# Neighbourhood attention in a two-layer diffusion backbone: value products of two blocks side by side, TensorE in the order of the code, projections spread over the blocks

## The chip, the core and the metric

The kernel runs on one core of one Trainium2 chip. The core has engines that run beside each other, each with its own queue of instructions, kept in step by semaphores: TensorE (PE; its weight loads stand in the profile as PEld), VectorE (DVE), ScalarE (ACT), GpSimd (POOL) and SyncE (SP), which here only issues DMAs. The metric is the device time of one execution in microseconds (us), lower is better. Three runs of the kernel before gave 2879.36, 2881.08 and 2881.36 us, median 2881.08 us.

## What is computed

The reference is a backbone of two layers over 1024 latent tokens (a grid of 16 rows and 64 columns) and 256 context tokens, width 1024. Each layer mixes tokens in two groups of eight heads, an mLSTM and a neighbourhood attention, and then has an MLP. The change touches the neighbourhood attention alone:

```python
def row_block(r):
    rs = jnp.clip(r - kr_n // 2, 0, rows - kr_n)          # 8 rows of keys
    q_r = lax.dynamic_index_in_dim(qg, r, axis=2, keepdims=False)
    k_r = lax.dynamic_slice_in_dim(kg, rs, kr_n, axis=2)
    v_r = lax.dynamic_slice_in_dim(vg, rs, kr_n, axis=2)
    s_loc = einsum(q_r, k_r) + bias                        # 16 columns of keys each
    s_ctx = einsum(q_r, kch)                               # and all 256 context tokens
    p = softmax(concatenate([s_loc, s_ctx], -1))
    return einsum(p_loc, v_r) + einsum(p_ctx, vch)
```

In the first layer the 256 context tokens also attend among themselves (`need_ctx`); in the last layer they do not.

## The kernel before

All products are fp32, or fp32 split into a high and a low half, so that a product with a weight matrix is three matmuls (`mm3`, lines 84 to 88: high by high, high by low, low by high). A projection of one group of tokens (`qk_project`, lines 704 to 710) is 8 steps over the width of three matmuls each, so 24 matmuls; the context group has 256 columns, each of the two latent groups 512.

**Blocks.** The attention goes through the heads in four pairs (`pr` 0 to 3). A latent block is 128 queries (8 rows by 16 columns) of both heads of a pair; its keys are the 256 context tokens and a window of 11 or 12 rows by 24 or 32 columns. A pair of heads has 8 latent blocks, and in the first layer 2 context blocks ahead of them: 10 blocks a pair there, 8 in the second layer, 72 in all.

**A block's three steps** (`na_block`, lines 845 to 905, a generator with two `yield`s):

1. Scores. PE: 4 matmuls against the context keys (line 853) and 4 against the window (line 863). DVE takes them out of PSUM with a running minimum of the negated scores (lines 858 and 864; 864 adds the bias that a DMA put into the tile `S`). ACT does the exponential and the row sum (868), DVE the reciprocal (869) and the scaling (870).
2. Transposes. PE turns the probabilities: 4 for the context (878), 4 and 2 for the window (889, 897). ACT copies the first and the last out of PSUM (879, 898), DVE the middle ones (890, tile `pl`).
3. Values. PE: 10 matmuls (904), each with 64 columns of weights, the two heads into the two halves of one PSUM bank. DVE copies the result out (784, or 761 for a context block; tile `nyT`).

**The order of the code.** `na` (lines 816 to 843) keeps two blocks pending. For each new block it asks for the transposes of the older pending one, then for the new block's scores, then for one step of `nxt`, and then for the values of the oldest block. `nxt` is the next pair's `na_qk` (712 to 746): a step of it is one projection of keys or queries of one group, 6 steps in the first layer and 5 in the second, taken one a block until none is left. For the last pair `nxt` is `ahead` (790 to 805): four steps that load and split output weights and load attention results, two that load residuals, and four output tiles of 24 matmuls. PSUM has 8 banks: 2 for projections (`mm`), 6 for all else (`q`), and each block takes 6 of the latter in turn.

**What sets the order on the engines.** The code's order is only what a scheduler starts from: before the program is built it reorders the instructions of every engine by estimated times, so that pieces of a projection may stand between a block's steps. A tile's buffers are handed round; a DMA into `S` (6 buffers, line 772) or into `vt` (the values of a window, line 776) is issued by SP, in SP's own order, when the last reader of that buffer is done.

## Time and profile before

The profiled execution has a span of 2883.5 us on its one core; it is 2.4 us above the median of the three runs without profile.

| engine | busy us | instructions |
|---|---|---|
| PE (matmuls) | 2833.7 | 16644 |
| PEld (weight loads) | 2402.4 | 16644 |
| DVE | 2216.7 | 5097 |
| ACT | 1262.9 | 2426 |
| POOL | 67.3 | 117 |

The attention stage runs from 457 to 688 us in the first layer and from 1963 to 2181 us in the second, 449 us in all. How to read it: an engine's busy time says little here about what sets the end, since PE's matmuls are pipelined and their ends are modelled. The sharper reading is the distance from the start of one matmul to the start of the next in the timeline. A timeline row gives start, time until the last of the merged instructions ended, engine, line, operation, output<-inputs, shape and count; `128*64 128x128` means 64 columns of weights.

### The profile page before, as it was taken

What the parts mean: (1) busy time and instruction counts of PE and PEld (TensorE: products, weight loads), DVE (VectorE), ACT (ScalarE), POOL (GpSimd) and SP (SyncE); (2) the same over time, 40 slices, a digit from 0 to 9 for tenths busy, and PEclk for the clock granted to TensorE, in tenths of its full rate; (3) what the DMA queues carried; (4) which work ended last, traced back from release to release, by engine and by line L of the source; (5) the groups of instructions that cost most, each with busy time, mean ns of one, the idle gap of its engine ahead of it and who ended that gap; (6) DMA issues with size and microseconds to landing.
All of it is one profiled execution on the core that took longest, in us unless ns stands there. A gap on an engine that the chain in (4) does not pass through costs nothing. (4 is left out here: it accounts for less than half of the span.)

```text
span 2883.5 us, 45724 instructions
## 1 busy us (share of the span) xinstructions
PE 2833.7 (98%) x16644; PEld 2402.4 (83%) x16644; DVE 2216.7 (77%) x5097; ACT 1262.9 (44%) x2426; POOL 67.3 (2%) x117
## 2 busy tenths in 40 slices
PE   8999999999999999999999999999999999999998
PEld 5888888888888888888889988888878788888888
DVE  7789987885798777599877778877786887759774
ACT  5333334564553333344544333335565533334453
POOL 0000000001000000000000000000010000000000
PEclk9999999999999999999999999999999999999999
DMA  7433332246447555798977222223256454478673
GB/s 248 164 123 105 113 115 78 91 125 217 150 157 235 188 197 198 273 334 288 313 260 252 67 88 73 74 62 105 88 169 199 132 190 144 154 252 312 212 252 102
DMA packets 278946, 497.42 MB, mean 173 GB/s; under 512 B 23328, under 2 KB 119584, under 8 KB 278720
## 3 DMA queue, kind: packets, MB, share of 16 engines
q1 hardware_dynamic: 278720, 494.49, 51.7%
q8 instruction: 131, 2.15, 0.3%
q14 instruction: 95, 0.78, 0.1%
HBM read 398.82 MB, written 95.59 MB: 171 GB/s over the span
## 5 line engine op out<-in xcount | busy, mean ns | idle before, releaser
L86 PE MATMUL q<-ah,whi 128*128 128x512 f32 (+1 forms) x1480 | 551.8, 373 | 2.6 <-ACT ah L955 1.9
L88 PE MATMUL q<-ah,wlo 128*128 128x512 f32 (+1 forms) x1480 | 550.2, 372 | 1.3 <-DVE wlo L956 1.3
L87 PE MATMUL q<-al,whi 128*128 128x512 f32 (+1 forms) x1480 | 550.7, 372 | 0.0
L86 PE MATMUL mm<-ah,whi 128*128 128x512 f32 (+1 forms) x1112 | 382.8, 344 | 1.5 <-ACT ah L914 1.5
L87 PE MATMUL mm<-al,whi 128*128 128x512 f32 (+1 forms) x1112 | 382.4, 344 | 0.4 <-DVE al L915 0.4
L88 PE MATMUL mm<-ah,wlo 128*128 128x512 f32 (+1 forms) x1112 | 382.1, 344 | 0.5 <-DVE wlo L81 0.5
L86 PEld LDWEIGHTS q<-ah,whi 128*128 128x128 f32 x1480 | 278.8, 188 | 52.3 <-ACT ah L955 2.7
L88 PEld LDWEIGHTS q<-ah,wlo 128*128 128x128 f32 x1480 | 278.8, 188 | 51.3 <-DVE wlo L956 2.1
L87 PEld LDWEIGHTS q<-al,whi 128*128 128x128 f32 x1480 | 278.9, 188 | 48.9 <-issue 1.4
L86 PE MATMUL mm<-whi,ah 128*128 128x512 f32 (+2 forms) x864 | 313.3, 364 | 0.9 <-DVE st L312 0.4
L87 PE MATMUL mm<-wlo,ah 128*128 128x512 f32 (+2 forms) x864 | 309.5, 359 | 0.2 <-DVE wlo L81 0.2
L88 PE MATMUL mm<-whi,al 128*128 128x512 f32 (+2 forms) x864 | 308.2, 357 | 0.0
L86 PEld LDWEIGHTS mm<-ah,whi 128*128 128x128 f32 x1112 | 210.5, 189 | 27.9 <-ACT ah L914 1.9
L88 PEld LDWEIGHTS mm<-ah,wlo 128*128 128x128 f32 x1112 | 210.6, 189 | 25.6 <-DVE wlo L81 1.0
L87 PEld LDWEIGHTS mm<-al,whi 128*128 128x128 f32 x1112 | 210.5, 189 | 25.0 <-DVE al L915 0.5
L955 ACT CAST ah<-raw 128x512 fp32r<-128x512 f32 (+1 forms) x264 | 142.9, 566 | 120.7 <-PE q L88 58.3
L86 PEld LDWEIGHTS mm<-whi,ah 128*128 128x128 f32 x864 | 163.6, 190 | 28.0 <-issue 3.1
L88 PEld LDWEIGHTS mm<-whi,al 128*128 128x128 f32 x864 | 163.8, 190 | 23.0 <-issue 0.7
L87 PEld LDWEIGHTS mm<-wlo,ah 128*128 128x128 f32 x864 | 163.9, 190 | 22.3 <-DVE wlo L81 0.4
L956 DVE TENSOR_TENSOR al<-raw,ah 128x512 fp32r<-128x512 f32 (+1 forms) x264 | 157.6, 621 | 23.5 <-ACT ah L955 23.0
L956 DVE TENSOR_TENSOR wlo<-raw,whi 128x1024 fp32r<-128x1024 f32 x84 | 102.4, 1222 | 74.4 <-ACT whi L955 71.9
L86 PE MATMUL q<-th,whi 128*128 128x512 f32 x384 | 150.5, 392 | 2.2 <-DVE s L1120 2.0
(287 smaller groups left out, 5249.4 us busy)
## 6 DMA issues: line engine op xcount, KB each, us to landing
raw<-w SPq DMA_DIRECT2D x168, 512.0 KB
raw<-hid SPq DMA_DIRECT2D x104, 512.0 KB
wada<-w_adaT SPq DMA_DIRECT2D x96, 512.0 KB
wraw<-w SPq DMA_DIRECT2D x80, 512.0 KB
hid<-hb SPq DMA_DIRECT2D x128, 256.0 KB
hid<-ht SPq DMA_DIRECT2D x96, 256.0 KB
gb<-gscr SPq DMA_DIRECT2D x36, 512.0 KB
wada<-w_ada SPq DMA_DIRECT2D x32, 512.0 KB
```

Source lines behind the costliest of these rows:

```text
L86: mm(out, lh, rh, start=start, stop=False, skip_group_check=True)
L87: mm(out, lh, rl, start=False, stop=False, skip_group_check=True)
L88: mm(out, ll, rh, start=False, stop=stop, skip_group_check=True)
L955: ins = self.nc.scalar.copy(hi, src)
L956: self.nc.vector.tensor_sub(lo, src, fview(hi))
```

## The change

The order of the code in the attention is new, and on PE it is kept as written:

- `na_pairs` goes through the blocks two by two. While the two blocks of a pair are scored, each scoring is preceded by the transposes of one block of the pair behind; when both are scored, the values of both blocks behind are asked for, one after the other (20 matmuls in one run).
- It runs under `manual_schedule` for PE: PE's instructions keep the code's order. DVE, ACT, POOL and SP are still ordered by the scheduler.
- A step of the next pair's projections is taken where `(n + 1) * parts // blocks` grows: in the first layer with the blocks n = 1, 3, 4, 6, 8, 9 (of 0 to 9), in the second with n = 1, 3, 4, 6, 7 (of 0 to 7). Before, these were the first 6 and the first 5 blocks. In the last pair `nxt` is stepped as before: the output tiles come with n = 8 and 9 in the first layer, 6 and 7 in the second, and at the end.
- `vt` has 5 buffers in place of 3.

```diff
-                vt = np_.tile([128, 3, 128], F32, name="vt", bufs=3)
+                vt = np_.tile([128, 3, 128], F32, name="vt", bufs=5)
...
-        pending = []
+        with self.tc.manual_schedule(engines={mybir.EngineType.PE}):
+            self.na_pairs(l, hi, lo, need_ctx, last)
+
+    def na_pairs(self, l, hi, lo, need_ctx, last):
+
+        behind, pair = [], []
+        parts, blocks = (6, 10) if need_ctx else (5, 8)
         for pr in range(4):
             nxt = self.na_qk(l, pr + 1, hi, lo, need_ctx) if pr < 3 else last
             for n, blk in enumerate(self.na_blocks(l, pr, need_ctx)):
-                if len(pending) == 2:
-                    next(pending[0])
+                if behind:
+                    next(behind[n % 2])
                 next(blk)
-                pending.append(blk)
-
-                if pr < 3 or not need_ctx or n > 1:
+                pair.append(blk)
+
+                if (n + 1) * parts // blocks > n * parts // blocks if pr < 3 else not need_ctx or n > 1:
                     next(nxt, None)
-                if len(pending) > 2:
-                    run_all(pending.pop(0))
+                if len(pair) == 2:
+                    for b in behind:
+                        run_all(b)
+                    behind, pair = pair, []
             if pr < 3 or not need_ctx:
                 run_all(nxt)
-        for blk in pending:
+        for blk in behind:
             next(blk)
-        for blk in pending:
+        for blk in behind:
             next(nxt, None)
             run_all(blk)
         run_all(nxt)
```

The instructions are the same on every engine, and outside the two attention stages so is their order. In the changed kernel the lines behind this place stand 8 further down (878 is 886, 889 is 897, 897 is 905, 853 is 861, 863 is 871, 904 is 912, 858 is 866, 864 is 872, 869 is 877, 870 is 878, 890 is 898).

**PE in the last pair of heads of the first layer.** Before, one block's values (three rows, 904) stand between pieces of transposes, and pieces of an output tile (`mm`) lie between:

```order
L88 MATMUL mm<-ah_5080,wlo 128x256
L878 MATMUL q<-consts,S 128x128
L904 MATMUL q<-pc,vc 64x128 x4
L904 MATMUL q<-pl,vt 64x128 x4
L904 MATMUL q<-pl_7935,vt 64x128 x2
L878 MATMUL q<-consts,S 128x128 x3
L889 MATMUL q<-consts,S 96x128 x4
L897 MATMUL q<-consts,S 72x128 x2
L853 MATMUL q<-nk_6791,nq 128x256 x2
L853 MATMUL q<-nk_6792,nq 128x256 x2
L863 MATMUL q<-nk_6791,nq 128x384 x2
L863 MATMUL q<-nk_6792,nq 128x384 x2
```

On the same engine at the same place of the changed kernel, the last rows of a block's transposes, the scores, and then the values of two blocks:

```order
L897 MATMUL q<-consts,S 128x128 x4
L905 MATMUL q<-consts,S 96x128 x2
L861 MATMUL q<-nk_6831,nq 128x256 x2
L861 MATMUL q<-nk_6832,nq 128x256 x2
L871 MATMUL q<-nk_6831,nq 128x264 x2
L871 MATMUL q<-nk_6832,nq 128x264 x2
L912 MATMUL q<-pc,vc 64x128 x4
L912 MATMUL q<-pl,vt 64x128 x4
L912 MATMUL q<-pl_7786,vt 64x128 x2
L912 MATMUL q<-pc,vc 64x128 x4
L912 MATMUL q<-pl,vt 64x128 x4
L912 MATMUL q<-pl_7852,vt 64x128 x2
```

The values of two blocks now follow each other, transposes come in whole blocks of 10, and no piece of an output tile stands between. Over both layers the values came in 75 runs before (72 blocks, three of them cut in two) and come in 37 now.

**DVE at the same place.** Before, between two copies of transposes (890), on the engine that hands the probabilities to PE's transposes (870):

```order
L890 COPY pl<-q 96x512
L870 TENSOR_SCALAR S<-S,ssum 128x544
L869 RECIPROCAL ssum<-ssum 128x1
L858 ISA S,smax<-q,zero 128x256
L858 ISA smax 128x1
L870 TENSOR_SCALAR S<-S,ssum 128x544
```

After, the same piece on DVE, here for the window of 264 (line 878 is the old 870):

```order
L898 COPY pl<-q 128x512
L866 ISA S,smax<-q,zero 128x256
L866 ISA smax 128x1
L877 RECIPROCAL ssum<-ssum 128x1
L866 ISA S,smax<-q,zero 128x256
L866 ISA smax 128x1
L878 TENSOR_SCALAR S<-S,ssum 128x520
```

The second scaling of a pair's second block now stands behind the copy of the first block's transposes and behind both minima of the next block's context scores.

**DVE at the head of the first layer's stage.** Before, the projection weights of the next pair are split (81) ahead of the first two scalings:

```order
L81 TENSOR_TENSOR wlo<-wraw,whi 128x1024
L745 TENSOR_TENSOR nq<-mm,nq 64x512 x2
L869 RECIPROCAL ssum<-ssum 128x1 x2
L730 SCALAR_TENSOR_TENSOR nk_5257<-mm,nk_5257 64x256
L870 TENSOR_SCALAR S<-S,ssum 128x256 x2
```

After, on the same engine, the split and two subtractions of queries stand between the third and the fourth scaling of the two context blocks:

```order
L745 TENSOR_TENSOR nq<-mm,nq 64x512 x2
L877 RECIPROCAL ssum<-ssum 128x1 x3
L878 TENSOR_SCALAR S<-S,ssum 128x256 x3
L877 RECIPROCAL ssum<-ssum 128x1
L81 TENSOR_TENSOR wlo<-wraw,whi 128x1024
L745 TENSOR_TENSOR nq<-mm,nq 64x512 x2
L878 TENSOR_SCALAR S<-S,ssum 128x256
```

The fourth scaling, which the second block's transposes need, has moved behind the split.

## Prediction

> **What bounds the kernel now.** I read the page's totals first, then the busy time by stretches of the attention stage, then the timeline of PE there.

> ```profile
> span 2883.5 us, 45724 instructions
> PE 2833.7 (98%) x16644; PEld 2402.4 (83%) x16644; DVE 2216.7 (77%) x5097; ACT 1262.9 (44%) x2426; POOL 67.3 (2%) x117
> 457.00:617.00 160.00, 158.30 (x1207) 136.43 (x1205) 122.80 (x384) 92.23 (x210) 3.69 (x5) 1.00 0.31 93
> 617.00:688.00 71.00, 66.75 (x663) 58.44 (x664) 57.12 (x204) 43.17 (x105) 10.53 (x9) 1.00 0.46 137
> 1963.00:2120.00 157.00, 154.88 (x1195) 133.05 (x1194) 121.94 (x366) 88.92 (x188) 7.80 (x6) 1.00 0.37 112
> 2120.00:2181.00 61.00, 58.32 (x483) 48.28 (x481) 47.28 (x146) 33.13 (x72) 1.41 (x1) 1.00 0.44 136
> ```

> PE is busy 98% of the span, so it sets the time nearly everywhere. The last four rows (length, then busy time of PE, PEld, DVE, ACT, POOL, granted clock, DMA share, GB/s) cut the two attention stages into the part with projections and the last pair of heads. PE idles 1.70, 4.25, 2.12 and 2.68 us in them, 10.75 us in 449 us. A change of order can win that much idle time at most; what else it can win must lie inside PE's busy time, in how fast the matmuls follow each other.

> **The change, part 1: fewer runs of value products.** Here is PE through one block, between two projections:

> ```profile
> 547.98 0.39 PE L87 MATMUL mm<-al,whi 128*128 128x512 f32 x1
> 548.20 0.39 PE L88 MATMUL mm<-ah,wlo 128*128 128x512 f32 x1
> 548.52 0.66 PE L904 MATMUL q<-pc,vc 128*64 128x128 f32 x8
> 549.01 0.83 PE L904 MATMUL q<-pl,vt 96*64 96x128 f32 x12
> 549.77 0.66 PE L878 MATMUL q<-consts,S 128*128 128x128 f32 x4
> 550.26 0.60 PE L889 MATMUL q<-consts,S 128*128 128x128 f32 x4
> 550.70 0.38 PE L897 MATMUL q<-consts,S 128*96 128x128 f32 x2
> 550.84 0.71 PE L853 MATMUL q<-nk,nq 128*128 128x256 f32 x4
> 551.39 0.64 PE L863 MATMUL q<-nk,nq 128*128 128x264 f32 x4
> 551.87 0.39 PE L86 MATMUL mm<-ah,whi 128*128 128x512 f32 x1
> ```

> And here the end of the second layer's stage, where transposes follow a projection and the values of two blocks already stand in one run:

> ```profile
> 2176.12 0.39 PE L88 MATMUL mm<-ah,wlo 128*128 128x512 f32 x1
> 2176.35 0.60 PE L878 MATMUL q<-consts,S 128*128 128x128 f32 x4
> 2176.79 0.60 PE L889 MATMUL q<-consts,S 128*128 128x128 f32 x4
> ...
> 2178.63 0.66 PE L904 MATMUL q<-pc,vc 128*64 128x128 f32 x8
> 2179.11 0.83 PE L904 MATMUL q<-pl,vt 128*64 128x128 f32 x12
> 2179.77 0.61 PE L904 MATMUL q<-pc,vc 128*64 128x128 f32 x8
> ```

> The reader is to compare starts. A projection's matmul takes 548.20 - 547.98 = 0.22 to 0.23 us, but the value products begin 0.32 us after the last one: **0.09** lost at the entry. The 12 records of line 904 take 2179.77 - 2179.11 = 0.66 us when another block's values follow (0.11 a pair of records), but 549.77 - 549.01 = 0.76 when transposes follow: **0.10** at the exit. The first 8 records take 549.01 - 548.52 = 0.49 where four pairs at 0.11 are 0.44: **0.05** on the first pair. Four transposes take 0.49 right behind values (549.77 to 550.26), 0.44 behind a projection (2176.35 to 2176.79): **0.05** more. And a projection goes over into transposes at no price (2176.12 to 2176.35 is 0.23). So each run of value products costs 0.29 us beside its products, whatever its length; the price goes with the change of shape (64 columns of weights against 128), not with the block. The runs fall from 75 to 37, by the order of the instructions: 38 x 0.29 = **-11.0 us**. All of it is on PE, which sets the time, as long as no wait takes its place.

> **Part 2: the last pair of heads, where no projection stands between blocks.** There PE ends its turn sooner than DVE:

> ```profile
> 652.58:656.39 3.81, 3.81 (x43) 3.50 (x42) 3.81 (x17) 2.42 (x6) 0.00 (x0) 1.00 0.32 97
> 656.39:660.23 3.84, 3.84 (x41) 3.43 (x41) 3.52 (x17) 2.38 (x6) 0.00 (x0) 1.00 0.72 203
> 658.76 0.69 DVE L890 COPY pl<-q 128x512 f32<-128x512 f32 x1 [0.17 <-PE q L889]
> 659.37 0.48 DVE L870 TENSOR_SCALAR S<-S,ssum 128x520 f32<-128x520 f32 x1
> 659.77 0.15 DVE L869 RECIPROCAL ssum<-ssum 128x1 f32<-128x1 f32 x1
> 659.84 0.40 DVE L858 CUSTOM_DVE_ANT_0 S<-q,zero 128x256 f32<-128x256 f32 x1
> 660.17 0.08 DVE L858 DVE_READ_ACCUMULATOR2_ANT smax<- 128x1 f32 x1
> 660.17 0.48 DVE L870 TENSOR_SCALAR S<-S,ssum 128x520 f32<-128x520 f32 x1
> 660.57 0.51 DVE L864 CUSTOM_DVE_ANT_0 S<-q,S,smax 128x288 f32<-128x288 f32 x1
> ```

> The first two rows are two turns of a block, 7.65 us together, with DVE busy 3.81 and 3.52. PE's own work for a block is 548.52 to 551.87 = 3.35 us with the smallest window, 0.1 more on average (0.48 us of it, 551.39 to 551.87, are four matmuls of 264 columns, and the windows have 322 on average), and the entry of 0.09: two blocks are about 7.1 us, and 6.8 with one run of values fewer. The wait that is late next is this. In the changed order on DVE, the last scaling of a pair's second block stands behind the copy `pl` of the first block's transposes and both context minima of the next block. From the start of those transposes: 0.49 until line 889 starts, 0.5 until it has ended (550.26 + 0.60), `pl` 0.61 to the next start, minimum 0.33, reciprocal 0.07, minimum 0.33, scaling 0.48: 2.9 us. PE arrives after the transposes and scores, 551.87 - 549.77 = 2.1 us. So PE waits **0.8 us** once a pair, behind it in PE's queue stand the scores of the next block and the pair's values, and for those DVE waits in turn; 6.8 + 0.8 is the 7.65 of DVE, both ways agree. Such pairs are three in each layer (blocks 2 to 7, and 0 to 5): 6 x 0.8 = 4.8 us of idle time. Before, pieces of output tiles filled part of it; in the code's order these come with the last two blocks, where they cover.

> **Part 3: elsewhere.** With a projection in the pair, PE has 6.8 us and 24 x 0.23 = 5.5 us more (half of that, 2.8, for the context group: an estimate from its width), at least 9.6 us, against DVE's 7.65 and at most four subtractions of queries and one split of weights:

> ```profile
> L745 DVE TENSOR_TENSOR nq<-mm,nq x52: 682/689/695, 459.3 to 2125.8; 64x512 fp32r<-64x512 f32 x52
> L81 DVE TENSOR_TENSOR wlo<-wraw,whi 128x1024 fp32r<-128x1024 f32 (+2 forms) x90 | 107.7, 1199 | 52.0 <-ACT whi L80 50.4
> PE q L878 <- DVE S L870: 1.1, 1, 1.1
> PE mm L86 <- ACT ah L914: 1.5, 1, 1.5
> DVE S L864 <- DMA S<-rpbt: 0.9, 2, 0.5
> ```

> 4 x 0.69 + 1.2 is 4.0 us, so a pair of DVE can reach 11.6 us, but the neighbouring pairs have 12 us of PE or more. The spread ends the four (three) blocks without cover that each pair of heads had; I cost it at nothing, and the range below takes it from -3 (most of the first and third stretch's idle time, 3.8 us, goes) to +3.

> At the head of each layer's stage the first transposes come sooner behind the scores. The wait of 1.1 us that is there in the first layer stays, and the fourth context scaling now stands behind a split and two subtractions, 1.2 + 1.4 us, of which PE covers the scores in between, 1.0: about 1.5 more. In the second layer two projections stood between the first scores and the first transposes, now one of 2.8 us: 1.5 to 2. Sum of idle time after: heads 2.6 + 2.0, last pairs 4.8, the wait for `ah` at the second layer's end 1.5 as before, 0.3 rest: 11.2 in place of 10.75, **+0.5 us**.

> The loads: `S` of a pair's second block can start when the block three back is transposed; without the value products in between that is one block's values (1.2 us) nearer to its use. The rows have 0.9 us of such waits in one stage; six pairs without cover bound it by 0 and 6 x 0.5 = 3 us on DVE. I take 0, being nearest to the row. With 3 buffers `vt` would now wait for values a pair later, with 5 it does not; SP's queue is otherwise as long as before. PSUM: until a run of values ends, two of the six `q` banks hold sums in place of one. No row shows a wait for a bank by name; the bounds are 0 and 0.5 us (a copy such as `pl`) in each of 36 pairs, 18 us. I take 0, since in the six pairs it hides in DVE's own period and in the others 2 us of slack lie before it.

> Sum: 2883.5 - 11.0 + 0.5 = 2873.0 us of span. The span is 2.4 us above the median of the runs, so 2881.1 - 10.5 = **2870.6 us**.

> [...] The granted clock in these rows is 1.00. The rows of an earlier place show what waits can do:

> ```profile
> 1620.00:1640.00 20.00, 17.71 (x130) 17.03 (x129) 15.92 (x18) 8.10 (x13) 1.48 (x4) 0.91 0.29 93
> 1625.96 0.44 PE L310 MATMUL mm<-consts,gr 128*128 128x128 f32 x2 [1.53 <-ACT kva L486]
> ```

> Three waits, 2.3 us in all within 4 us, and the clock's mean over 20 us falls to 0.91: 1.8 us lost. [...]

> **The rivals.**

> - *The gain is mostly eaten* (2878.5 us). PE in fixed order cannot step over a late transpose; 0.25 us of bank or softmax waits in each of 30 pairs is 7.5 us. For it: two banks held, DVE at 3.8 us a block. Against: 2 us of slack in every pair with a projection. Chance 0.20.
> - *Slower* (2889 us). The mechanism: DVE's order, laid by estimated times, puts a copy of values (784) ahead of the scalings that PE's next transposes need, so that each pair waits for its own values: a copy and a scaling, 0.3 + 0.5 us, in all 36 pairs, 29 us less what cover there is, 10: +19 - 10.5. It decides from 0.3 us a pair upwards. Chance 0.08.
> - *Clock* (2876 us). Waits at a stage's head join to over 2.3 us and the clock falls once or twice, 1.8 us each, with the wait itself 2. Chance 0.02.
> - *Better* (2863.5 us). The spread also removes the idle time of parts 2 and 3: -11.0 and some 6.5 of the 10.75. Chance 0.20.
> - *It does not do what it says*: the order of PE shows the 37 runs, and transposes uncut. Chance 0.

> **How the numbers follow.** Forecast 2870.6, chance 0.50, by its terms 2866 to 2876. Some 0.2% of this kernel, 5.8 us, is what a measurement can tell from no change: the line is 2875.3. Faster: 0.49 of the forecast, 0.20 of the better case, 0.05 of the eaten one: 0.74. Within: 0.01, 0.14 and the clock 0.02: 0.17. Slower: 0.01 of the eaten case and 0.08: 0.09. The range 2861.5 to 2880 leaves out the slower case and the outer parts of the better and the eaten one, under 2 in 10.

> **What would show it.** Right: value runs of 40 records with 1.14 us a block in the inside; transposes at 0.44 behind projections; the two stages 231 + 218 shorter by 10 in all; PE's waits at the transposes about 0.8 us in six pairs. Wrong: waits at line 886 or 897 in pairs that hold a projection (banks or DVE's order), PE idle above 15 us in the stages, or a first row in the list of waits that names `nyT`.

## The result, and the profile after

The changed kernel takes 2896.57 us (median of 6 runs, 2893.83 to 2905.72) beside 2881.22 us for the kernel before on the same chip (6 runs, 2877.96 to 2885.06). The ratio is 1.0055, with a 95% interval of 1.0041 to 1.0070: slower, by 15.4 us in the medians, where 10.5 us less were predicted. The time lies outside the predicted range.

The page of the changed kernel, its first lines, and the busy time by stretches (columns as in the prediction: length, then PE, PEld, DVE, ACT, POOL, granted clock, DMA share, GB/s). The stretches are the first layer's projected pairs of heads and its last pair, then the second layer's head, its projected pairs and its last pair:

```profile
span 2895.4 us, 45645 instructions
PE 2834.4 (98%) x16644; PEld 2410.9 (83%) x16644; DVE 2215.6 (77%) x5097; ACT 1266.2 (44%) x2426; POOL 68.5 (2%) x117
```

```profile
457.00:617.00 160.00, 157.65 (x1281) 139.61 (x1280) 127.48 (x415) 95.63 (x218) 2.18 (x3) 1.00 0.31 95
617.00:690.60 73.60, 65.54 (x596) 58.09 (x595) 53.37 (x177) 44.56 (x102) 12.20 (x11) 0.98 0.47 141
1963.00:1980.00 17.00, 14.04 (x87) 12.13 (x86) 15.69 (x55) 11.76 (x25) 0.00 (x0) 0.90 0.33 97
1980.00:2115.00 135.00, 133.49 (x1050) 115.60 (x1049) 100.47 (x309) 71.17 (x153) 2.63 (x2) 1.00 0.33 99
2115.00:2195.00 80.00, 70.73 (x546) 60.39 (x545) 53.50 (x153) 40.73 (x81) 7.54 (x5) 0.94 0.43 139
```

PE idles 2.35, 8.06, 2.96, 1.51 and 9.27 us: 24.15 us, where it was 10.75 before and 11.2 were forecast. And the clock, 1.00 in all of both stages before, is below 1 in three of these rows: 73.60 x 0.02, 17 x 0.10 and 80 x 0.06 are 8 us of clock. Most of both lies in the last pairs of heads and at the head of the second layer. The first layer's projected stretch is nearly free of idle time behind its head: from 466 to 628 us PE idles 0.3 us in 162.

What PE waits for in each stage of the changed kernel (us in total, times, longest):

```profile
PE q L886 <- DVE S L878: 6.5, 5, 3.1
PE q L905 <- ACT pc L887: 1.2, 1, 1.2
PE q L871 <- DVE smax L872: 1.0, 1, 1.0
PE q L871 <- ACT pc L887: 0.7, 1, 0.7
...
PE q L871 <- ACT pc L887: 5.0, 2, 2.8
PE q L886 <- DVE S L878: 3.7, 3, 1.6
PE mm L86 <- ACT ah L922: 1.6, 1, 1.6
PE q L905 <- ACT pc L887: 1.2, 4, 0.3
```

Two names carry it: transposes (886) that wait for the last scaling of a softmax (878), which the prediction had in its sum at 0.8 us each, and scores or transposes (871, 905) that cannot write their PSUM bank until ACT has copied the transposes out of it (887). Neither kind of matmul reads `pc`; what ties them to it is the bank that the copy empties. The second group is 8.1 us in the rows shown, and the prediction had it at nothing.

### The profile page after: what moved, and what is told of

It reads as the page before. It is cut to its first block, busy times and chain, and to the rows that moved or that the text cites. A ratio compares the mean times of both kernels' runs of the same rounds, so it can differ in the third digit from the quotient of the medians.

```text
span 2895.4 us, 45645 instructions
## 1 busy us (share of the span) xinstructions
PE 2834.4 (98%) x16644; PEld 2410.9 (83%) x16644; DVE 2215.6 (77%) x5097; ACT 1266.2 (44%) x2426; POOL 68.5 (2%) x117
## 5 line engine op out<-in xcount | busy, mean ns | idle before, releaser
L86 PE MATMUL q<-ah,whi 128*128 128x512 f32 (+1 forms) x1480 | 551.9, 373 | 1.0 <-ACT ah L963 0.9
L87 PE MATMUL q<-al,whi 128*128 128x512 f32 (+1 forms) x1480 | 551.0, 372 | 0.3 <-DVE al L964 0.3
L88 PE MATMUL q<-ah,wlo 128*128 128x512 f32 (+1 forms) x1480 | 550.3, 372 | 0.9 <-DVE wlo L964 0.7
L86 PE MATMUL mm<-ah,whi 128*128 128x512 f32 (+1 forms) x1112 | 383.1, 344 | 1.6 <-ACT ah L922 1.6
L87 PE MATMUL mm<-al,whi 128*128 128x512 f32 (+1 forms) x1112 | 382.5, 344 | 0.2 <-DVE al L923 0.2
L88 PE MATMUL mm<-ah,wlo 128*128 128x512 f32 (+1 forms) x1112 | 382.2, 344 | 0.4 <-DVE wlo L81 0.4
L88 PEld LDWEIGHTS q<-ah,wlo 128*128 128x128 f32 x1480 | 278.9, 188 | 50.4 <-DVE wlo L964 1.7
L86 PEld LDWEIGHTS q<-ah,whi 128*128 128x128 f32 x1480 | 278.9, 189 | 50.2 <-ACT ah L963 1.4
L87 PEld LDWEIGHTS q<-al,whi 128*128 128x128 f32 x1480 | 279.0, 189 | 49.7 <-issue 1.4
L86 PE MATMUL mm<-whi,ah 128*128 128x512 f32 (+2 forms) x864 | 313.3, 364 | 0.8 <-DVE st L312 0.4
L87 PE MATMUL mm<-wlo,ah 128*128 128x512 f32 (+2 forms) x864 | 309.6, 359 | 1.2 <-DVE wlo L81 1.2
L88 PE MATMUL mm<-whi,al 128*128 128x512 f32 (+2 forms) x864 | 308.1, 357 | 0.0
L86 PEld LDWEIGHTS mm<-ah,whi 128*128 128x128 f32 x1112 | 211.2, 190 | 27.9 <-ACT ah L922 2.0
L88 PEld LDWEIGHTS mm<-ah,wlo 128*128 128x128 f32 x1112 | 211.1, 190 | 25.7 <-DVE wlo L81 0.8
L87 PEld LDWEIGHTS mm<-al,whi 128*128 128x128 f32 x1112 | 211.1, 190 | 25.1 <-DVE al L923 0.5
L86 PEld LDWEIGHTS mm<-whi,ah 128*128 128x128 f32 x864 | 163.6, 190 | 28.0 <-issue 3.1
L87 PEld LDWEIGHTS mm<-wlo,ah 128*128 128x128 f32 x864 | 163.9, 190 | 23.2 <-DVE wlo L81 1.4
L88 PEld LDWEIGHTS mm<-whi,al 128*128 128x128 f32 x864 | 163.7, 189 | 23.0 <-issue 0.7
L964 DVE TENSOR_TENSOR al<-raw,ah 128x512 fp32r<-128x512 f32 (+1 forms) x264 | 157.7, 621 | 23.9 <-ACT ah L963 23.4
L81 DVE TENSOR_TENSOR wlo<-wraw,whi 128x1024 fp32r<-128x1024 f32 (+2 forms) x90 | 107.7, 1198 | 60.5 <-ACT whi L80 47.6
```

What stands on the lines that cost most here:

```text
L81: nc.vector.tensor_sub(lo[:, :n], raw[:, :n], fview(hi[:, :n]))
L86: mm(out, lh, rh, start=start, stop=False, skip_group_check=True)
L87: mm(out, lh, rl, start=False, stop=False, skip_group_check=True)
L88: mm(out, ll, rh, start=False, stop=stop, skip_group_check=True)
L964: self.nc.vector.tensor_sub(lo, src, fview(hi))
```

## Where a wait comes from

PE, ACT and SP of the changed kernel around the longest wait of the second layer, at the last block of its third pair, on the way into the last pair (a row's bracket: idle time before it, and what ended it):

```profile
2116.60 0.42 PE L871 MATMUL q<-nk,nq 128*128 128x288 f32 x2
2119.86 0.85 PE L871 MATMUL q<-nk,nq 128*128 128x288 f32 x2 [2.84 <-ACT pc L887]
2120.51 0.63 PE L86 MATMUL mm<-ah,whi 128*128 128x512 f32 x1
```

```profile
2117.09 1.04 ACT L80 CAST whi<-wraw 128x1024 fp32r<-128x1024 f32 x1 [3.87 <-DMA wraw<-w_out]
2118.04 0.57 ACT L742 CAST nq<-mm 64x512 fp32r<-64x512 f32 x1
2118.62 0.58 ACT L743 CAST nq<-mm 64x512 fp32r<-64x512 f32 x1
2119.23 0.58 ACT L887 COPY pc<-q 128x512 f32<-128x512 f32 x1
```

ACT stands 3.87 us before the split of the second of the four output weights, because its load has not landed. Two casts of queries and then the copy that PE needs are queued behind that split. PE's own queue is now in code order, so it stands too: behind the waiting scores is a whole projection (line 86), which needs nothing and may not pass. When PE goes on, its matmuls take 0.43 us from start to start (0.63 each) in place of 0.23: the granted clock is 0.50 there. The wait is not the order's alone: e1 below, where the scheduler orders PE, stands 2.2 us for the same copy.

The load itself starts late. (The expectations below call it the first; the first of the four is loaded at 1996.5.) SP's queue, the changed kernel and then the kernel before:

```profile
2112.46 0.33 SPq L73 DMA_DIRECT2D wraw<-w_out  x1
```

```profile
2095.15 0.33 SPq L73 DMA_DIRECT2D wraw<-w_out  x1
```

From the first score of the stage (1963.8 and 1963.5 in the timeline) that is 148.7 us in place of 131.6.

## The experiments

All runs in one table. Ratio: to the kernel before on the same chip, with its 95% interval. Runs: of value products, in both layers. Stage 1, 2: from the first score to the last value product of a layer, in the timeline of the profiled run. Half clock: time within the two stages in which the granted clock is 0.5, in that run; at 0.43 us from matmul to matmul in place of 0.23, as above, each 3.4 us of it costs up to 1.7. The last three columns come from one execution each.

| kernel | ratio (95%) | runs | stage 1 | stage 2 | half clock |
|---|---|---|---|---|---|
| before | 1 | 75 | 232.0 | 218.0 | 0 |
| the change | 1.0055 (1.0041-1.0070) | 37 | 233.7 | 231.0 | 17.0 |
| e1_free_order | 1.0011 (1.0001-1.0020) | 54 | 230.3 | 219.4 | 3.4 |
| e2_single_fixed | 1.0051 (1.0036-1.0066) | 71 | 239.0 | 223.3 | 3.4 |
| e3_no_spread | 1.0070 (1.0054-1.0085) | 37 | 240.1 | 223.3 | 3.4 |
| e4_act_fixed | 1.0444 | 37 | 287.7 | 283.4 | 116 |
| e5_last_free | 1.0056 (1.0037-1.0075) | 53 | 231.4 | 227.0 | 6.8 |
| e6_only_last | 1.0027 (1.0015-1.0039) | 37 | 234.9 | 222.6 | 17.1 |
| e7_sb8 | 1.0055 (1.0038-1.0073) | 37 | 234.6 | 226.0 | 13.7 |
| e8_split_pool | 1.0060 (1.0039-1.0080) | 37 | 237.9 | 228.7 | 23.9 |
| e9_free_nospread | 1.0005 (0.9995-1.0014) | 61 | 232.5 | 216.3 | 0 |
| e10_free_early_out | 1.0017 (1.0009-1.0026) | 48 | 234.4 | 218.9 | 10.2 |
| e11_spread_first_layer | 1.0008 (0.9999-1.0017) | 57 | 230.9 | 215.7 | 0 |
| e12_output_after | 1.0083 (1.0066-1.0099) | 36 | 229.7 | 209.6 | 30.7 |
| e13_no_load_wait | 1.0034 (1.0023-1.0046) | 37 | 231.9 | 221.1 | 10.2 |
| e14_no_load_free | 0.9982 (0.9973-0.9992) | 51 | 230.9 | 212.5 | 3.4 |
| e15_other_queue | 1.0071 (1.0057-1.0085) | 37 | 237.9 | 232.2 | 20.5 |
| e16_other_queue_free | 1.0024 (1.0015-1.0033) | 52 | 234.3 | 221.7 | 6.8 |

**Which part of the change costs.** First the change without its fixed order, then the fixed order without the rest, then pairs without the spread:

```diff
# e1_free_order, against the change
-        with self.tc.manual_schedule(engines={mybir.EngineType.PE}):
-            self.na_pairs(l, hi, lo, need_ctx, last)
+        self.na_pairs(l, hi, lo, need_ctx, last)
# e2_single_fixed, against the kernel before
+        with self.tc.manual_schedule(engines={mybir.EngineType.PE}):
             pending = []
...
# e3_no_spread, against the change
-                if (n + 1) * parts // blocks > n * parts // blocks if pr < 3 else not need_ctx or n > 1:
+                if pr < 3 or not need_ctx or n > 1:
```

> Pairs, spread projections and 5 value buffers as in the change, but PE is again ordered by the scheduler; it keeps runs of two blocks nearly everywhere outside the last pair of heads (54 runs of values against 37 and 75). Theory A (the fixed order of PE costs: it cannot step over transposes and scores that wait for ACT and DVE in the last pair of heads, and its long waits lower the clock): about 2875 us, 21 x 0.29 = 6 us under before, waits as before. Theory B (going two by two costs, since two banks hold sums and loads come late, whoever sets the order): 2890 us or more.

> The kernel before, one block at a time, projections first and 3 value buffers, with nothing but the fixed order of PE added. Theory A: slower than before by the 26 us of waits that the change added, less what single blocks are spared: 2895 to 2905 us. Theory B: as before, 2881 us, within 4.

> The change with the projections again in the first blocks of each pair of heads (fixed order, two by two). If the spread covers waits (prediction, part 3): three more stretches without projection in each layer, 10 waits of 0.8 us more, so 2900 to 2908 us. If the spread does nothing: 2896 us, as the change.

The order alone, on the kernel before, costs as much as the whole change (1.0051); without it most of the loss is gone (1.0011), but none of the forecast gain is there. (By the price of a run, 21 runs fewer are 6.1 us; e1's two stages are 0.3 us shorter. What took the rest was not isolated.) What e2 waits for in the first layer's stage:

```profile
PE q L905 <- ACT pl L899: 7.6, 8, 1.6
PE mm L86 <- DVE nq L745: 3.2, 1, 3.2
```

With one block at a time in code order, the values (905) follow the transposes whose copy (899) ACT has still to make, eight times in this stage. Pairs take that wait away, and the runs fall from 71 to 37; e3, where the pairs are made and the projections not spread, is no faster for it (stages of 463.4 us in sum, 462.3 in e2). The spread then helps the first layer (240.1 to 233.7) and harms the second (223.3 to 231.0). Without the order it does the same on a smaller scale (e9 against e1: 232.5 to 230.3, and 216.3 to 219.4).

**ACT in code order too.**

```diff
-        with self.tc.manual_schedule(engines={mybir.EngineType.PE}):
+        with self.tc.manual_schedule(engines={mybir.EngineType.PE, mybir.EngineType.Activation}):
```

> The change, with ACT in the order of the code as well as PE, so that no split of output weights, which waits for its DMA, stands ahead of the copy of a transpose that PE waits for. Theory A1 (the long waits come from what the scheduler put ahead on ACT): the waits for pc (some 9 us) and half of the clock's losses go, 2882 to 2887 us. Theory A2 (they come from DVE and the loads): no gain, 2893 to 2900 us.

In code order a split of weights stands right ahead of the projection that needs it, so PE waits 3.3 to 7.9 us before each, 51 us in twelve waits; the clock is at half for 116 us. It says how much the scheduler's early splits are worth, and nothing on the change.

**Where in the stage the order costs.**

```diff
# e5_last_free; e6_only_last has pr == 3
+            return self.tc.manual_schedule(engines={mybir.EngineType.PE}) if pr < 3 else nullcontext()
...
+            with order(pr):
```

> The changed kernel, with TensorE in code order only in the pairs of heads that project the next pair's queries and keys (the first three of each layer); the last pair of heads and the drain of each layer are left to the scheduler. Theory A (the order costs where nothing but blocks is left to run and one late engine holds all of TensorE: of the 43 us that TensorE waits in the two stages of the changed kernel, 10 + 14 us lie in the last pairs, with three of the four clock drops, some 6.8 us): the last pairs fall back to about 9 us of waits in all and no clock drop, so some 20 us less than the changed kernel, ratio to before 0.997 to 1.000, 2876 to 2885. Theory B (the order costs about alike in all pairs): 25 to 30 per cent of the loss comes back, ratio 1.003 to 1.005, 2893 to 2898.

> The mirror: TensorE in code order only in the last pair of heads and the drain of each layer, the first three pairs left to the scheduler; pairs of blocks and spread projections kept. Theory A: nearly as slow as the change, ratio 1.003 to 1.008, 2893 to 2907, with the waits for the copy of line 887 and for the softmax in the last pairs. Theory B: near the change without the order (1.0011), ratio 1.000 to 1.003.

I expected nearly all of it in the last pairs, and that is wrong. Against e1 the two stages are 8.7 us longer with the first three pairs ordered and 7.8 us longer with the last ones ordered; the ratios, 1.0056 and 1.0027 beside 1.0011, put more on the first three pairs, with wide intervals. The 8.7 lie at few places. The largest is the head of the second layer, here in the changed kernel, and then in e6, where the scheduler orders it:

```profile
1971.06 0.94 PE L871 MATMUL q<-nk,nq 128*128 128x352 f32 x4
1973.58 0.44 PE L886 MATMUL q<-consts,S 128*128 128x128 f32 x2 [1.58 <-DVE S L878]
1975.15 0.44 PE L886 MATMUL q<-consts,S 128*128 128x128 f32 x2 [1.13 <-DVE S L878]
```

```profile
1973.97 0.82 PE L873 MATMUL q<-nk,nq 128*128 128x352 f32 x4
1974.62 0.39 PE L88 MATMUL mm<-ah,wlo 128*128 128x512 f32 x1
...
1976.30 0.44 PE L888 MATMUL q<-consts,S 128*128 128x128 f32 x2
```

The scheduler puts the next projection (lines 86 to 88) between the scores and the transposes that wait; the code has it behind the next block's transposes and scores (1978.17). With the half clock that follows, the place costs some 5 us: from the first score to the first value product it is 1963.85 to 1984.27 here, 20.4 us, and 1966.56 to 1982.02, 15.5 us, in e6. The starts of the second and third pair of that layer cost some 2 more.

And e6 shows where e1's runs are cut: it has 37 runs itself. In the first three pairs the scheduler by itself leaves the values of a pair together. The cuts that bring e1 to 54 runs are all in the last pairs, where it fills waits with values.

**What the last pairs wait for.** More buffers for the tables; the output weights' split on GpSimd; the same loads two steps earlier; the output projection behind the blocks:

```diff
# e7_sb8
-SB = 6
+SB = 8
# e8_split_pool, for the output weights that run ahead
-        nc.scalar.copy(hi[:, :n], raw[:, :n])
-        nc.vector.tensor_sub(lo[:, :n], raw[:, :n], fview(hi[:, :n]))
+        (nc.gpsimd.tensor_copy if pool else nc.scalar.copy)(hi[:, :n], raw[:, :n])
+        (nc.gpsimd if pool else nc.vector).tensor_sub(lo[:, :n], raw[:, :n], fview(hi[:, :n]))
# e10_free_early_out, against e1
+                if pr == 2 and n in (6, 8 if need_ctx else 7):
+                    next(last)
# e12_output_after, against the change
-                if (n + 1) * parts // blocks > n * parts // blocks if pr < 3 else not need_ctx or n > 1:
+                if pr < 3 and (n + 1) * parts // blocks > n * parts // blocks:
...
-            if pr < 3 or not need_ctx:
+            if pr < 3:
                 run_all(nxt)
```

> The changed kernel with eight S buffers in place of six, so that two blocks' tables can be loaded ahead, not one. Theory C (late tables: the 3.1 us wait at 643.8 of the changed kernel ends with a softmax that started on a table that landed 1.6 us late): the waits of the softmax for the S load go and 3 to 6 us come back, ratio 1.003 to 1.0045. Rival (the queue of the loads is itself behind, or ACT is what is late): under 2 us, ratio 1.005 to 1.006.

> The changed kernel with the split of the output weights in the last pair (both halves) on GpSimd in place of ACT and DVE, so that ACT's copies of the transposes no longer stand behind a split that waits for its load (2.0 us in the first layer, 3.9 us in the second). Theory D (that head-of-line wait on ACT is the main cause in the last pairs): the waits of 2.8 and 2.2 us at line 871 for the copy of line 887 and of 1.4 and 0.6 us at 634 go, with a clock drop or two, 6 to 11 us in all, ratio 1.0015 to 1.0035, 2889 to 2895. Rival (ACT is late by the y loads and the exponentials too, or the slower split delays the output tiles): 0 to 3 us, ratio 1.0045 to 1.006, or slower than the change.

> The change without the order, spread kept, with the first two steps of the output projection's loads and splits two steps earlier: inside the third pair of heads, behind the projection of its queries, in place of the start of the last pair. Theory E: the first loads start some 8 us earlier in each layer, the waits behind ACT's split at 632.5 and 2108.2 go with the clock drop, 4 to 7 us less than the change without the order, ratio 0.9985 to 1.0000, 2881 to 2885. Rival F: the waits move elsewhere, ratio 1.0005 to 1.0025, 2886 to 2892.

> The changed kernel (TensorE in code order) with the output projection's loads, splits and tiles begun only behind the last block of each layer, so that the last pair of heads holds nothing but blocks. The whole gets longer by the loads that now stand bare behind the stage (four weights and eight y tiles, 10 to 30 us in each layer by the 2 to 4 us that one is waited for), so the verdict is read within the last pairs. Theory G (ACT stands behind the loads of the output weights and of y, and the copies and exponentials of the blocks behind it): TensorE's waits in the last pairs, up to the last value product, fall from 10 and 14 us to under 5 each, and the waits at 871 and 905 for the copy of line 887 go. Rival H (the blocks' own chain of softmax, transposes and copies is longer than two blocks' products in this order): the waits stay at 8 us or more in each, at the transposes for the second scaling, with clock drops.

None of the four brings anything back. In e7 the wait on the way into the second layer's last pair is still there (2.6 us for the copy). In the first layer's last pair, which e7 was aimed at, the tables `S` still come late. This is the changed kernel there, DVE and PE:

```profile
644.87 0.49 DVE L872 CUSTOM_DVE_ANT_0 S<-q,S,smax 128x264 f32<-128x264 f32 x1 [1.55 <-DMA S<-rpbt]
647.08 0.44 PE L886 MATMUL q<-consts,S 128*128 128x128 f32 x2 [3.05 <-DVE S L878]
```

With eight buffers DVE waits 0.85 and 0.86 us for the two tables, and PE 2.16 us in place of 3.05. So the buffers are not what holds them, or not alone: in the changed kernel SP is at nine loads of `vt` from 630.60 to 640.20 before the next loads of `S`. No run changes the number of `vt`'s buffers alone, so their part stays open.

The other three do no better. In e8 GpSimd waits for the load instead, up to 7.4 us, and ACT still stands before the casts of y (17.0 us in eleven waits between 615 and 700 us). In e10 and e12 the edit did not reach its aim: the loads and ACT's splits are placed by the scheduler and stayed where they were. In e10 the second weight's load starts 149.4 and 141.8 us into the stages, as in e1 (149.3 and 141.8). In e12 only PE's output tiles moved; ACT in it, at the same place:

```profile
2127.04 1.04 ACT L80 CAST whi<-wraw 128x1024 fp32r<-128x1024 f32 x1 [3.65 <-DMA wraw<-w_out]
...
2129.18 0.59 ACT L886 COPY pc<-q 128x512 f32<-128x512 f32 x1
```

PE waits 2.62 us for that copy (2.84 in the change). So e12 does not tell the loads from the blocks' own chain. The next two do, in part: the loads that run ahead are left out, and the engines do the same work on a tile that is loaded at the stage's head.

```diff
# e13_no_load_wait; e14_no_load_free is the same on e1
+        self.fixed = self.np_.tile([128, 1024], F32, name="fixed", bufs=1)
+        self.nc.sync.dma_start(self.fixed[:], self.d["w_out"][l, 0])
...
-        for i, _ in enumerate(self.w_out(l, 0, W)):
-            self.load_y(l, gi, yh, yl, range(2 * i, min(2 * i + 2, KT - 1)))
+        for i in range(WB):
+            W.append(self.split_raw(self.fixed, 1024))
+            self.load_y(l, gi, yh, yl, range(2 * i, min(2 * i + 2, KT - 1)), self.fixed)
```

> The changed kernel (TensorE in code order), where the weights and the y tiles of the output projection that runs ahead are taken from one tile that is loaded at the head of the stage: all splits, casts and products of it stay where they were, only their loads (four weights and eight y tiles in each layer) are left out, and the result of that projection is not the reference's. Theory G (ACT, and DVE behind it, stand behind these loads, with the copies and exponentials of the blocks behind them): the waits for the copy of line 887 at the head of the last pairs (1.2 and 0.3 us at 634, 2.8 us at 2117, 2.2 us at 2140) and the clock drops next to them go; the two stages' waits by start-to-start fall from 43 us to 25 or less, ratio 0.998 to 1.0015. Theory H (the blocks' own chain in this order): the last pairs keep 8 us or more of waits each, stages less than 8 us shorter, ratio 1.003 to 1.005.

> The same without the loads, TensorE left to the scheduler (pairs and spread kept). Theory G: the waits of 2.0 us at 632.5 and 2.4 us at 2108.2 of that kernel with loads, and its clock drop, go; ratio 0.996 to 0.999, and the order costs less than the 13 us that it costs with the loads (5 to 8 us, the heads of the stages). Theory H: ratio 1.000 to 1.002, the order costs as much as with the loads.

The answer differs by layer. In the second, the stage is 9.9 us shorter than in the change, and the 5.0 us of scores waiting for the copy (line 890 here) are gone from its waits; what stays is mostly the head and the starts of pairs:

```profile
PE q L889 <- DVE S L881: 3.5, 3, 1.6
PE q L864 <- DVE smax L875: 2.1, 3, 0.7
PE q L908 <- ACT pc L890: 1.2, 4, 0.3
```

In the first layer it is 1.8 us shorter only: there the last pair keeps 3.5 us of waits for scalings after 622 us and 1.1 us for a copy, though these loads are gone. (The tables `S` are still loaded, and DVE waits 0.36 and 0.53 us for two of them at 646.08 and 648.56.) But the splits did not stay where they were, as I had expected: with their tile always there, the scheduler has ACT make the second and third of the second layer 106.8 and 140.3 us into the stage, where the change has them at 153.2 and 164.6. So e13 takes work out of the last pair as well as waits, and its gain is not the waits' alone. Without the order the loads cost as much or more: 0.9982 against 1.0011. But the order costs no less when these loads are gone (e13 over e14: 0.0052, with loads 0.0044). So the loads, with the places of the splits that hang on them, and the order are two losses side by side; the loads explain a part of the second layer at most.

**Why the loads are late.**

```diff
# e15_other_queue: the output weights that run ahead; e16_other_queue_free is the same on e1
-        for i, _ in enumerate(self.w_out(l, 0, W)):
+        for i, _ in enumerate(self.w_out(l, 0, W, self.nc.gpsimd)):
```

> The changed kernel with the four output weights that are loaded during the last pair issued on GpSimd's queue in place of SyncE's, where they stand behind loads of S and vt that wait for buffers. Theory Q (SyncE's queue is what makes those weights late): the first weight of the second layer starts some 8 us or more before 2112.5, ACT's waits for w_out (2.0 us, 3.9 and 1.7 us) go or shrink to under 1 us, and with them the waits of 2.8 and 2.2 us for the copy of line 887 and two or three clock drops, 5 to 9 us in all, ratio 1.002 to 1.004. Rival R (the load waits for one of the two wraw buffers, whatever queue it stands in, or GpSimd's own subtractions hold it): the loads start where they did, ratio 1.005 to 1.007.

> The same on the change without the order (pairs, spread, TensorE left to the scheduler; 1.0011). Theory Q: 3 to 6 us less than that, ratio 0.9985 to 1.000, near the 0.9982 of the same kernel without these loads. Rival R: ratio 1.0005 to 1.0025.

SP's queue is not the reason. On GpSimd's queue the second weight's load starts at 2120.9 in the second layer, 149.4 us into the stage (148.7 in the change), and ACT waits 4.5 us for it. Neither kernel is faster (1.0071 beside 1.0055, 1.0024 beside 1.0011; the intervals overlap).

What holds the load can be read from the traces. Weights and attention results (y) are loaded into the two buffers of `wraw` in turn. In the change, two y tiles that SP loads at 2022.1 and 2051.0 hold both buffers until ACT has cast the first of them into `ah` and GpSimd has subtracted. First the change, then the kernel before:

```profile
2110.44 0.62 ACT L922 CAST ah<-wraw 128x512 fp32r<-128x512 f32 x1 [1.11 <-PE mm L88]
2111.14 1.29 POOL L923 TENSOR_TENSOR al<-wraw,ah 128x512 fp32r<-128x512 f32 x1 [175.49 <-DMA vt<-vscr]
```

```profile
2093.14 0.62 ACT L914 CAST ah<-wraw 128x512 fp32r<-128x512 f32 x1 [1.22 <-PE mm L88]
2093.83 1.29 POOL L915 TENSOR_TENSOR al<-wraw,ah 128x512 fp32r<-128x512 f32 x1 [158.49 <-ACT ah L914]
```

The cast overwrites an `ah` that a projection still reads, and waits for that projection's first step on PE. The subtraction ends at 2112.43 and 2095.12, and the weight's load is issued at 2112.46 and 2095.15; in e15 the same three steps stand at 2118.59, 2119.30 and 2120.88. So the load is tied to a projection that the spread has moved: 17.3 us later, as the load is. Without the spread, in e9, the load starts 129.9 us into the second layer's stage. No run cuts this chain by itself.

**The best mixture.**

```diff
# e9_free_nospread, against e1
-                if (n + 1) * parts // blocks > n * parts // blocks if pr < 3 else not need_ctx or n > 1:
+                if pr < 3 or not need_ctx or n > 1:
# e11_spread_first_layer, against e1
+                if (n + 1) * parts // blocks > n * parts // blocks if pr < 3 and need_ctx else not need_ctx or n > 1 or pr < 3:
```

> Pairs of blocks and the deeper value buffers alone: TensorE left to the scheduler, projections in the first blocks as in the kernel before. Theory E (spreading moves the first load of an output weight behind the late projections: it starts at 606.0 and 2103.6 in the change without the order, 598.5 and 2095.2 before, and ACT's split of that weight then waits 2.6 and 3.7 us for the load with the copies of the next pairs' queries behind it): the waits of 2.0 us at 632.5 and of 2.4 us at 2108.2 with its clock drop go, the saving of fewer runs of value products stays (75 to about 54 runs, 21 x 0.29 = 6 us), ratio 0.997 to 0.9995, 2876 to 2884 beside 2885. Rival F (pairing itself makes the waits, since two blocks' softmaxes then fall together): ratio 1.000 to 1.003, 2885 to 2894.

> Pairs of blocks with TensorE left to the scheduler, projections spread in the first layer only (there the stage took 230.3 us with the spread and 232.5 without), in the first blocks in the second layer (216.3 without, 219.4 with the spread). If the two stages add as measured: 446.6 us against 450.0 before, ratio 0.998 to 0.9995, 2880 to 2885 beside 2886. Rival: the stages change with where the clock drops fall, and the rest of the program is not the same either; ratio 1.000 to 1.0015.

The stages add as expected (230.9 + 215.7 = 446.6, 3.4 us less than before), but the time does not follow: 1.0008. No complete version was faster than the kernel before; pairs of blocks, left to the scheduler, are level with it.

## Why the prediction was wrong

**Part 1, the price of a run, was right where it can be read.** The changed kernel at the end of a projected pair:

```profile
628.85 0.39 PE L88 MATMUL mm<-ah,wlo 128*128 128x512 f32 x1
629.17 0.66 PE L912 MATMUL q<-pc,vc 128*64 128x128 f32 x8
629.65 0.83 PE L912 MATMUL q<-pl,vt 96*64 96x128 f32 x12
630.31 0.61 PE L912 MATMUL q<-pc,vc 128*64 128x128 f32 x8
630.75 0.82 PE L912 MATMUL q<-pl,vt 128*64 128x128 f32 x12
631.51 0.66 PE L886 MATMUL q<-consts,S 128*128 128x128 f32 x4
```

Entry 0.32 in place of 0.23, the first block 630.31 - 629.17 = 1.14, the last twelve products 0.76 with the exit: the terms of the sum, once for two blocks. Over both stages, each matmul's undisturbed distance to the next, with these switches, adds up by my count to 434.2 us before and 422.7 after, some 11 less where 11.0 were forecast; what is taken as undisturbed moves this difference by a few us. The runs are 37.

**Part 2, the last pairs without projections, was wrong.** The 0.8 us at the transposes of a pair's second block is there (beside the longest one, two waits of 1.4 us in sum in the first layer's last pair). But 4.8 us were forecast for both layers' last pairs, 6.3 with the wait for `ah`; PE idles 8.06 and 9.27 us in the two stretches. The step that failed is that these pairs were worked out from DVE's period alone, and everything DVE and ACT wait for was left at nothing. In the second layer it is ACT: what stands in its queue ahead of a block's copies, and which load that waits for (3.87 us, shown above). In the first layer the longest wait, 3.05 us, ends with a scaling whose table `S` came 1.55 us late: the loads of `S`, bounded by 3 us and taken at 0. (In the working of the 0.8, the term given as 0.5 is 0.60 by its rows, and the sum of 2.9 holds with that.)

**Part 3.** Its middle was right, and better than taken: the spread empties the projected stretches. The first layer's head was right (2.1 us idle from 457 to 466, forecast 2.6). The second layer's head was forecast at 2.0 and costs 2.96 idle and 1.7 by the clock. Two terms failed. "SP's queue otherwise as long as before" left out that a later end of the projections makes the next loads later: 17 us for the second output weight. And the PSUM banks were taken at 0 in a range of 0 to 18: the rows name waits for `pc` of 8.1 us in the changed kernel, since a bank is held until ACT comes to its copy. That no row of the kernel before shows a wait for a bank by name was a misreading; these two do, in the first layer's last pair and in the second layer's projected pairs:

```profile
PE q L863 <- ACT pc L879: 0.8, 2, 0.6
PE q L863 <- ACT pc L879: 0.9, 1, 0.9
```

**The clock** stood as a rival at a chance of 0.02 with one or two falls; there are five windows of 3.4 us at half speed in the stages, some 8 us. In the trace's record of the clock these are four stretches at 0.50, from 648.16, 1975.94, 2119.30 and 2143.20 us, three of 3.413 us and the last of 6.827. The granted clock of the changed kernel, in three places, each a window of 3.41 us and the one that follows it:

```profile
634.52:637.93 3.41, 2.23 (x26) 1.84 (x28) 3.32 (x9) 2.63 (x9) 0.73 (x1) 1.00 0.23 65
637.93:641.34 3.41, 3.32 (x41) 2.86 (x37) 3.41 (x19) 2.35 (x8) 0.00 (x0) 1.00 0.12 35
644.76:648.17 3.41, 0.56 (x3) 0.33 (x4) 3.30 (x17) 2.26 (x5) 0.00 (x0) 1.00 0.59 189
648.17:651.58 3.41, 3.41 (x16) 3.31 (x17) 2.65 (x11) 1.30 (x4) 0.00 (x0) 0.50 0.25 74
2115.87:2119.28 3.41, 1.15 (x10) 0.92 (x8) 1.12 (x1) 2.16 (x4) 0.00 (x0) 1.00 0.50 157
2119.28:2122.69 3.41, 2.83 (x8) 2.35 (x9) 3.33 (x9) 3.09 (x6) 1.28 (x1) 0.50 0.26 77
```

PE busy 0.56 or 1.15 of 3.41 us: the next window ran at 0.50. PE busy 2.23 of 3.41: it did not. So PE had worked for a third of a window (1.15 of 3.41 us) and the clock fell all the same.

**The sum.** In the stages: -11.0 for the runs, +13.4 of idle time by the rows (24.15 - 10.75), +8 by the clock: +10.4, where the timeline has 464.7 - 450.0 = +14.7. Part of the rest, 4.3 us, is in how idle time is counted: from the modelled end of a matmul, so that a wait is short by some 0.15 us (2116.60 to 2119.86 is 3.26 us, two matmuls of 288 columns take 0.26 by the 0.13 from one such matmul to the next at 71 us, so 3.00 are lost where the row says 2.84). Counted from start to start, what is left beside the undisturbed sum, waits and clock together, grows from 450.0 - 434.2 = 15.8 to 464.7 - 422.7 = 42.0 us. Outside the stages the span is 2.8 us shorter. That makes 2883.5 + 14.7 - 2.8 = 2895.4.

Of the rivals, the slower one named the right sign and the wrong place: `nyT` is nowhere near the top of the waits. The judgement "PE idle above 15 us in the stages" is what came true. And the rival that was missing is the one that e2 shows: the fixed order, with nothing else, costs 1.0051.

## What to carry to other kernels

An engine that is put in code order stops at the first late operand with ready work behind it that a scheduler would have put ahead (here PE for 2.84 us before 2119.86, with a whole projection ready), so price the order alone, on the unchanged kernel, before anything that is built on it; and for each queue that must then be in time, ACT's as well as DVE's, list what stands ahead of the needed instruction and which load that waits for. Spreading work to fill gaps also moves its end, and with it the start of what comes after: here the first layer won 6.4 us by it and the second lost 7.7. A saving inside an engine's busy time can be read from start-to-start distances, and still be worth nothing when the waits that it makes exceed it.
